# Triangular inverses on 32x32 array tiles, two units per direction in flight, in a one-core encoder layer

## The chip, the core and the metric

The kernel runs on one NeuronCore of a Trainium2 chip. The metric is device time in microseconds (us) of one execution. Engines are named as in the profile: PE (TensorE matmul) and PEld (its weight loads), DVE (VectorE), ACT (ScalarE), POOL (GpSimd), SP (SyncE, which issues the DMAs here).

## The reference

The layer normalises and modulates `x`, projects it once, and splits the projection between a dilated-window attention (three dilations, merged by their softmax denominators) and a bidirectional RWKV-7 time mixing. Both outputs are projected back, and a squared-ReLU feed-forward part follows. It is applied to 2048 prompt tokens and 256 sample tokens, with shared weights, in f32. The part that matters here is the recurrence, run forward and backward for 8 heads of 64:

```python
def _rwkv_step(state, inp):
    w, kk, b, k, v, r = inp
    sa = jnp.einsum('dbhvk,dbhk->dbhv', state, kk)
    state = state * w[..., None, :] - sa[..., :, None] * b[..., None, :] + v[..., :, None] * k[..., None, :]
    y = jnp.einsum('dbhvk,dbhk->dbhv', state, r)
    return state, y
```

The kernel does it in chunks of 64 tokens. Inside a chunk the dependence of each token on the earlier ones is a unit triangular 64x64 system, whose matrix is inverted; between chunks only the 64x64 state is handed on.

## The kernel before, in words

The program has three phases, one after the other: phase A (projection, token shift, decay), phase B (recurrence and attention, interleaved), phase C (output projection and feed-forward). Only phase B is changed. There is one stretch of phase B for each `c` of 0 to 3 (a pair of heads, in the two 64-partition halves).

A *unit* is 8 chunks of one direction `d` of one `c` (the sample tokens form units of 4 chunks): per `c` four units of 8 and one of 4 for each direction, 40 units in all. `units[::2]` are forward, `units[1::2]` backward. A *half* is 4 chunks of both directions; there are 36. For each unit the following run as separate streams, written as Python generators:

- `load_stream`: SP loads the tiles `kr` and `bk` (`NKR` and `NBK` buffers) of the unit.
- `prod_stream`: PE multiplies `bk` by `kr`, 64 partitions at a time (`hd` is the head), four chunks into one PSUM bank named `pb`; `mask_stream` copies it to the tile `x` on ACT, `gate_stream` masks it on POOL. There are `NX` tiles `x`, freed when the unit's chain is done.
- `prep_stream` calls `unit_prep`: the inverse. The 64x64 matrix is seen as 2x2 blocks of 32. Both diagonal blocks are inverted in f16 by five doubling levels (`for li in range(5)`), refined twice, and the off-diagonal block follows from two products in high and low parts. A level is: product on PE into `pb`, mask on DVE (`xs`), second product on PE, update of `t` on DVE, a DVE transpose of 32x32 blocks into `mc`. In each product four blocks (2 heads, 2 diagonal blocks) of each chunk are computed at once with a 128x128 operand that holds the four 32x32 blocks on its diagonal and zeros elsewhere. `spread` makes this operand: a DVE multiplication by a block mask that writes 128 columns per chunk from 32. Its outputs are `mb` and `mbl`; the operands `e32` and `eof`, filled from `x`, are kept spread as well. `low_stream` forms the low parts of these on POOL.
- At the end of `unit_prep` the tile `m` is written (`NLATE` buffers; it waits until the chain of the unit `NLATE` before is done, and `lock2` lets one unit at a time through), and a DMA puts another operand into `x`. Then the unit is marked `ready`.
- `late_load` and `late_gate`: for each half SP loads `rc` and `uv`; POOL scales `bk`, PE transposes it, ACT copies it to `bt`. There are `NH` sets.
- `chain_stream` calls `pair_chain`: 8 (or 4) steps for a forward and a backward unit together. A step is: products into the bank `pc` (`x,uv` and `rc,uv`), copy `rr` on ACT, product `rr,m`, copy into `uv` on ACT, products `uv,bt` and `uv,x`, then the new state on DVE (`uv<-pc,sw`). It starts when both units are `ready`; there are 144 steps.

One `prep_stream` per direction takes its units one after the other, so two inverses are in progress at a time. Beside all this `attn_stream` keeps up to six attention blocks in flight (`ps` scores, `pt` transposes, `pb` outputs), and `norm_stream` finishes the rows of `y`.

The order on each engine is fixed when the program is built. The class `Pace` keeps a model of when each engine is free, with a cost for each operation, and takes next the stream whose next operation can start first, plus a small amount times its progress. The engines then execute in that order and wait for semaphores. Where the model sees PE idle for long, `warm` adds products of the constant `bdh` whose results are overwritten (*fillers* below). The PSUM banks are: three `pb`, two `pc`, two `ps`, one `pt`.

## Time and profile before

| | us |
|---|---|
| median of 3 runs (lowest, highest) | 4227.92 (4219.04, 4238.62) |
| the profiled execution | 4239.46 |
| its span, first to last instruction | 4237.6 |
| first and last chain step in it | 1145.1, 2353.9 |

Mean granted PE clock over the span: 0.962. Over the span PE is busy 95%, DVE 62%, ACT 41%, POOL 35%. Matmuls overlap in a pipeline, and a matmul's busy time is that from its start to its modelled end: eight small products that start 25 ns apart count 0.35 us together, though one alone counts 0.17 us. So a busy PE is not one that could take no more. Nearly all operations are recorded by one helper, at line 117, so operations are told apart by their tile names, `out<-in`.

### The profile page before, as it was taken

The numbers are of one execution on the slowest core, as the hardware profiler recorded it, in microseconds if no ns is written. First come the engines' busy times: TensorE is split into PE (matmuls) and PEld (weight loads), VectorE is DVE, ScalarE is ACT, GpSimd is POOL, SyncE is SP. The second block draws the span as 40 slices with busy tenths as digits, with TensorE's granted clock in tenths as the row PEclk, the third lists the DMA queues.
The fourth block names the chain that finished last, engine by engine and source line by source line (L and its number), as shares of the span: only waits on it lengthen the run. The fifth ranks groups of instructions, "written<-read, shape, count | busy, mean of one in ns | idle before, by whom it ended". The sixth has DMA issues, their size and how long they took to land.

```text
span 4237.6 us, 76554 instructions
## 1 busy us (share of the span) xinstructions
PE 4035.7 (95%) x29994; PEld 3339.5 (79%) x29994; DVE 2606.8 (62%) x5429; ACT 1754.5 (41%) x4301; POOL 1484.1 (35%) x1471
## 2 busy tenths in 40 slices
PE   8989999998899999999999799999999999999997
PEld 5878789888566666666666588889999888889997
DVE  4898788788668768767667354444444464444445
ACT  5556556555565566566465322121221221112221
POOL 2553431211645645645544443112121141112123
PEclk9999999999899899899799899999999999999999
DMA  6566565454433323324222444111111141111112
GB/s 228 205 224 224 173 201 191 152 171 153 145 79 94 106 69 93 110 71 109 83 75 55 155 145 154 41 40 48 42 44 42 53 167 40 40 40 43 48 41 80
DMA packets 341674, 452.57 MB, mean 107 GB/s; under 512 B 152384, under 2 KB 237376, under 8 KB 340288
## 3 DMA queue, kind: packets, MB, share of 16 engines
q1 hardware_dynamic: 340480, 446.98, 32.8%
q8 instruction: 236, 3.87, 0.4%
q14 instruction: 126, 1.03, 0.1%
q10 hardware_dynamic: 832, 0.69, 0.1%
HBM read 319.90 MB, written 127.68 MB: 106 GB/s over the span
## 4 chain that ended last, share of the span: by engine, by line
PE 54%; DVE 4%; issue 1%; ACT 1%; POOL 1%; DMA 0%; POOLq 0%; SPq 0%; DVEq 0%; ACTq 0%
PE p L117 42%; PE pb L117 5%; PE pc L117 3%; PE ps L117 3%; PE pt L117 1%; DVE mb L117 1%; DVE m L117 0%; DMA mx<-scr_mix 0%; DVE uv L117 0%; DVE mc L117 0%; DVE t L117 0%; POOL ya L117 0%; POOL x L117 0%; DVE w L117 0%; DVE p L117 0%
## 5 line engine op out<-in xcount | busy, mean ns | idle before, releaser
L117 DVE TENSOR_TENSOR z<-z 128x384 f32<-128x384 f32 x192 | 190.2, 991 | 591.1 <-ACT gh L117 591.1
L117 DVE TENSOR_TENSOR ya<-ya,p 128x512 f32<-128x512 f32 x540 | 363.9, 687 | 277.5 <-PE p L117 276.5
L117 PE MATMUL pin<-hi,whi 128*128 128x386 f32 (+3 forms) x1512 | 499.4, 330 | 16.6 <-ACT praw L325 8.9
L117 PE MATMUL p<-hi,mh 128*128 128x384 f32 x1536 | 513.3, 334 | 0.0
L117 PE MATMUL p<-hi,ml 128*128 128x384 f32 x1536 | 513.2, 334 | 0.0
L117 PE MATMUL p<-lo,mh 128*128 128x384 f32 x1536 | 513.0, 334 | 0.0
L117 PE MATMUL pin<-hi,wlo 128*128 128x386 f32 (+3 forms) x1512 | 484.6, 320 | 6.3 <-POOL wlo L117 5.1
L117 PE MATMUL pin<-lo,whi 128*128 128x386 f32 (+3 forms) x1512 | 484.0, 320 | 1.2 <-DVE lo L117 1.2
L117 PE MATMUL p<-xn,gh 128*128 128x512 f32 x1152 | 458.9, 398 | 0.0
L117 PE MATMUL p<-mx,gh 128*128 128x512 f32 x1152 | 458.1, 398 | 0.5 <-DVE ya L117 0.5
L117 PE MATMUL p<-mx,gl 128*128 128x512 f32 x1152 | 452.1, 392 | 0.0
L117 POOL TENSOR_TENSOR xn<-x,mx 128x1024 fp32r<-128x1024 f32 x64 | 152.8, 2407 | 653.7 <-ACT mx L117 653.7
L117 ACT ACTIVATE mx<-x 128x1024 fp32r<-128x1024 f32 x64 | 64.3, 1052 | 694.6 <-PE p L117 694.6
L117 POOL TENSOR_TENSOR ml<-x,mh 128x1024 fp32r<-128x1024 f32 x64 | 153.8, 2403 | 556.1 <-ACT mh L117 556.1
L117 PEld LDWEIGHTS pin<-hi,whi 128*128 128x128 f32 x1512 | 292.2, 193 | 30.3 <-ACT praw L325 9.8
L117 PEld LDWEIGHTS pin<-hi,wlo 128*128 128x128 f32 x1512 | 292.6, 193 | 9.3 <-POOL wlo L117 7.0
L117 PEld LDWEIGHTS pin<-lo,whi 128*128 128x128 f32 x1512 | 293.3, 194 | 5.5 <-DVE lo L117 2.7
L117 PEld LDWEIGHTS p<-hi,mh 128*128 128x128 f32 x1536 | 288.3, 188 | 1.5
L117 PEld LDWEIGHTS p<-lo,mh 128*128 128x128 f32 x1536 | 288.3, 188 | 1.3
L117 PEld LDWEIGHTS p<-hi,ml 128*128 128x128 f32 x1536 | 288.3, 188 | 0.0
L117 PE MATMUL ps<-kz,q 128*128 128x512 f32 (+2 forms) x400 | 272.7, 775 | 0.8 <-DVE st L117 0.6
L117 PEld LDWEIGHTS p<-mx,gh 128*128 128x128 f32 x1152 | 215.8, 187 | 56.5 <-DVE ya L117 0.9
(303 smaller groups left out, 8895.8 us busy)
## 6 DMA issues: line engine op xcount, KB each, us to landing
x<-wff SPq DMA_DIRECT2D x128, 512.0 KB
whi<-scr_wp SPq DMA_DIRECT2D x54, 512.0 KB
wlo<-scr_wp SPq DMA_DIRECT2D x54, 512.0 KB
raw<-wada SPq DMA_DIRECT2D x83, 256.0 KB
scr_kr<-kr SPq DMA_DIRECT2D x48, 384.0 KB
scr_bk<-bk SPq DMA_DIRECT2D x48, 384.0 KB
x<-xp SPq DMA_DIRECT2D x32, 512.0 KB
kr<-scr_kr SPq DMA_DIRECT2D x32, 512.0 KB
```

What stands on the lines that cost most here:

```text
L117: return f(out, *a, **k)
```

## The change

It does five things. (1) The four 32x32 blocks of a chunk are no longer spread over a 128x128 operand: the new function `blocks` issues four products, each with a 32x32 stationary operand at the partitions of its block, and its output in the 32 partitions of the same block (or of the neighbouring one, `swap`). `spread`, `mb`, `mbl` and `lock2` go, and `e32` and `eof` have 32 columns a chunk. (2) There are four sets of the inverse's tiles (`u["set"]`), and four `prep_stream`s and `low_stream`s: two units of each direction can be in progress. (3) In `prod_stream` the products of the two heads alternate and fill two `pb` banks. (4) The tile `bk` is freed after these products; `late_gate` works on a tile `bkl` that `late_load` loads again for each half. (5) `NBK, NX, NH, NLATE` go from 3, 5, 3, 3 to 2, 6, 2, 4, and the model's costs know of the small tiles.

```diff
-            if b.dtype == FH:
-                return max(26.0, n / 2.4 + 3), n * rows
+            if b.dtype == FH:
+                return max(26.0, n / 2.4 + 3) * (0.4 if m == 32 else 1.0), n * rows
...
-        NKR, NBK, NX, NH, NLATE, NY = 1, 3, 5, 3, 3, 4
+        NKR, NBK, NX, NH, NLATE, NY = 1, 2, 6, 2, 4, 4
...
+        e32 = [[cp.tile([128, 8, 32], FH, name=f"e32{q}{i}") for i in range(4)] for q in range(2)]
+        eof = [[cp.tile([128, 8, 32], FH, name=f"eof{q}{i}") for i in range(4)] for q in range(2)]
...
                 for n0 in range(0, nn, 4):
+                    yield room("pb", NPB), room("pb", NPB - 1), "P"
+                    u[n0, 0], u[n0, 1] = pbank([128, 4, 128]), take(psB, [128, 4, 128], FT, "pb", NPB)
+                    for n in range(4):
+                        for hd in range(2):
+                            pr = slice(64 * hd, 64 * hd + 64)
+                            mm2(u[n0, hd][0][:, n], bk[pr, n0 + n, :], kr[pr, n0 + n, :], start=True, stop=True)
...
+                    yield room(f"bkl{d}", 1), "S"
+                    h["bkl", d] = take(su, [128, 4, 128], FT, f"bkl{d}", 1)
+                    dma_(h["bkl", d][0], S["bk"][c, d, :, n0:n0 + 4, :])
...
-            def spread(c32, mask, name):
-                z = su.tile([128, 8, 128], FH, name=name, bufs=1)
-                tt(z[:, :nn].rearrange("p n (b t) -> p n b t", b=4), c32[:, :nn, None, :].to_broadcast([128, nn, 4, 32]),
-                   mask[:, None].to_broadcast([128, nn, 4, 32]), OP.mult)
-                return z
...
+            def blocks(ps, w, swap, *pairs):
+
+                for n in range(nn):
+                    for z, (a, b) in enumerate(pairs):
+                        for q in range(4):
+                            r, o = slice(32 * q, 32 * q + 32), slice(32 * (q ^ swap), 32 * (q ^ swap) + 32)
+                            mm(ps[o, n, 0:w], a[r, n], b[r, n], start=z == 0, stop=z == len(pairs) - 1)
...
-                    for n in range(nn):
-                        mm(ps[:, n, 0:16], mb[:, n], xs[:, n], start=True, stop=True)
+                    blocks(ps, 16, 0, (mc, xs))
...
-            yield (lambda: late(u) and not lock2), at_(i - NLATE, "done")
-            lock2.append(i)
-            xlb = spread(xl, bdsw[:, d], "mbl")
-            yield
+            yield (lambda: late(u)), at_(i - NLATE, "done")
...
         def prep_stream(d):
-            for u in units[d::2]:
+            for u in units[d::4]:
...
+            for k in (d, d + 2):
+                pace.add(prep_stream(k), "prep", lambda d=k: prog[1, d] + BT["prep"])
+                pace.add(low_stream(k), "low", lambda d=k: prog[1, d] + BT["low"])
```

The order on DVE, in the middle of an inverse. `t` is the running inverse of a unit, `mc` its transpose, `xs` the masked product, `tpl` the low part in the last stage of the other unit; a number after a name is the buffer. Before:

```order
L117 SCALAR_TENSOR_TENSOR t_14491<-pb,t_14491 128x64x2
L117 STREAM_TRANSPOSE mc_14655<-t_14491 128x256
L117 TENSOR_TENSOR mb_14657<-mc_14655,bdh 128x1024
L117 SCALAR_TENSOR_TENSOR tpl_14637<-pb,tph_14636 128x256
L117 TENSOR_TENSOR mb_14669<-tph_14636,bdh 128x1024
L117 TENSOR_TENSOR mbl<-tpl_14637,bdh 128x1024
L117 TENSOR_TENSOR xs_14704<-pb,lvl 128x128
```

And now:

```order
L117 TENSOR_TENSOR xs_20276<-pb,lvl 128x128
L117 SCALAR_TENSOR_TENSOR m_20282<-t_19332,eyes 128x256
L117 SCALAR_TENSOR_TENSOR mph_20284<-pb,m_20282 128x256
L117 SCALAR_TENSOR_TENSOR o_11176<-o_11176,pv,pb 128x512
L117 SCALAR_TENSOR_TENSOR t_19865<-pb,t_19865 128x32x4
L117 STREAM_TRANSPOSE mc_20345<-t_19865 128x256
L117 TENSOR_TENSOR xs_20397<-pb,lvl 128x128
```

The multiplications by `bdh` into `mb` and `mbl` are gone; what follows a transpose is the next level's `xs` at once.

The order on PE, around a chain step (`rr,m`, then `uv,bt` and `x,uv`). Before:

```order
L117 MATMUL pc<-rr,m 64x64 x4
L117 MATMUL pb<-kr,bk 128x128 x4
L117 MATMUL pc<-uv,bt_13232 64x64 x2
L117 MATMUL pc<-uv,bt_13308 64x64 x2
L117 MATMUL pc<-x,uv 64x64 x4
L117 MATMUL pb<-kr,bk 128x128 x4
```

And now:

```order
L117 MATMUL pb<-kr,bk 128x128 x8
L117 MATMUL pc<-rr,m 64x64 x4
L117 MATMUL pb<-ident,bkl_33228 128x128 x4
L117 MATMUL pc<-uv,bt_32642 64x64 x2
L117 MATMUL pc<-uv,bt_32746 64x64 x2
L117 MATMUL pc<-x,uv 64x64 x4
```

The products `kr,bk` of the two heads, two groups of 4 that stood in different places of a step, are one group of 8.

The order on SP, at the loads for a half. Before:

```order
L181 DMA bk<-scr_bk 128x512
L181 DMA kr<-scr_kr 128x1024
L181 DMA rc_19246<-scr_kr 128x4x64
L181 DMA rc_19280<-scr_kr 128x4x64
L181 DMA vx<-scr_v 64x512
L181 DMA uv<-scr_vt 64x4x64 x4
```

And now:

```order
L185 DMA bkl_26335<-scr_bk 128x512
L185 DMA bkl_26428<-scr_bk 128x512
L185 DMA vx<-scr_v 128x512
L185 DMA rc_26334<-scr_kr 128x4x64
L185 DMA rc_26427<-scr_kr 128x4x64
L185 DMA x<-scr_kr 64x8x64
L185 DMA uv<-scr_vt 64x4x64 x4
```

Two loads `bkl` stand ahead of those of `rc` and `uv` of the same half.

## The prediction, as put on record before the change was run

> **What bounds the kernel now.** I read the chain's steps first, since only phase B changes and a chain of 144 steps runs through it. The copy `rr` on ScalarE occurs once a step, so its starts are the steps' clock. The first fence is the tile view of `rr` (count, durations in ns, first and last start in us), the second the ScalarE timeline over the end of one unit and around a change of `c`.

> ```profile
> L117 ACT ACTIVATE rr<-pc x144: 253/278/322, 1145.1 to 2353.9; 128x128 f32<-128x128 f32 x144
> ```

> ```profile
> 1414.64 0.28 ACT L117 ACTIVATE rr<-pc 128x128 f32<-128x128 f32 x1 [4.37 <-PE pc L117]
> 1440.03 0.27 ACT L117 ACTIVATE rr<-pc 128x128 f32<-128x128 f32 x1
> ...
> 1600.92 0.28 ACT L117 ACTIVATE rr<-pc 128x128 f32<-128x128 f32 x1
> 1610.31 0.26 ACT L117 ACTIVATE rr<-pc 128x128 f32<-128x128 f32 x1
> 1615.83 0.28 ACT L117 ACTIVATE rr<-pc 128x128 f32<-128x128 f32 x1
> 1621.46 0.28 ACT L117 ACTIVATE rr<-pc 128x128 f32<-128x128 f32 x1 [0.17 <-PE pc L117]
> 1634.98 0.28 ACT L117 ACTIVATE rr<-pc 128x128 f32<-128x128 f32 x1
> ```

> The steps take 2353.9 - 1145.1 = 1208.8 us, 8.45 us each. They are not even: within the unit the gaps are 5.5 to 9.4 us, into the next unit 13.5 us (1621.46 to 1634.98), into the next `c` 25.4 us. Summing the 143 gaps of these rows by kind, the 124 within units make 895 us (7.2 each) and the 19 into a next unit 314 us (16.5 each), of which the three into a next `c` (25.4, 31.1, 40.4) make 97. What is waited for at 1634.98 stands in the VectorE timeline of that stretch: the last operation of each inverse (`m<-pb,m`) and the first of the next (`COPY t<-eye`).

> ```profile
> 1607.65 0.39 DVE L117 SCALAR_TENSOR_TENSOR m<-pb,m 128x256 f32<-128x256 f32 x1
> ...
> 1613.66 0.19 DVE L117 COPY t<-eye 128x128 f16<-128x128 f16 x1
> ...
> 1628.32 0.42 DVE L117 SCALAR_TENSOR_TENSOR m<-pb,m 128x256 f32<-128x256 f32 x1
> ...
> 1635.28 0.15 DVE L117 COPY t<-eye 128x128 f16<-128x128 f16 x1
> ```

> The second unit's inverse ends at 1628.7, its last operand is then loaded into `x`, and the chain steps on at 1635. In each direction the next inverse starts only after the one before (1607.65 to 1613.66, 1628.32 to 1635.28). So the two inverses in progress run back to back and finish just before each pair of units can start: at unit boundaries the chain waits for the inverses. The stretch as a whole (windows view: busy us of PE, PEld, DVE, ACT, POOL, then granted clock, DMA share, GB/s):

> ```profile
> 1145.00:2354.00 1209.00, 1151.64 (x14616) 808.87 (x14615) 857.49 (x2699) 708.19 (x2313) 606.11 (x833) 0.93 0.31 85
> ```

> VectorE is busy 71%, ScalarE 59%, POOL 50%. PE's 95% counts pipelined latency.

> **The change, part by part.** The sum is made against the profiled execution, 4239.46 us, which lies 11.5 above the median.

> *Spreading goes.* These groups (lines view) vanish from VectorE:

> ```profile
> L117 DVE TENSOR_TENSOR mb<-mc,bdh 128x1024 f16<-128x1024 f16 (+1 forms) x160 | 127.3, 796 | 5.5
> L117 DVE TENSOR_TENSOR mbl<-tpl,bdh 128x1024 f16<-128x1024 f16 (+1 forms) x40 | 32.9, 822 | 0.1
> L117 DVE TENSOR_TENSOR mb<-mph,bdh 128x1024 f16<-128x1024 f16 (+1 forms) x40 | 29.2, 730 | 1.4
> L117 DVE TENSOR_TENSOR mb<-tph,bdh 128x1024 f16<-128x1024 f16 (+1 forms) x40 | 28.4, 709 | 0.0
> ```

> Together 217.8 us, 1.5 us of each chain step's 8.45, and 7 operations, about 5.4 us, of each inverse. VectorE is not the wait within steps, so this is not 218 us of time. Bounds for the 143 gaps: 0 and -215 (1.5 each).

> *Two units per direction.* An inverse that starts a unit earlier no longer ends last. I let the 16 ordinary boundaries fall from (314 - 97) / 16 = 13.6 us to a step within a unit, 7.2: 16 x 6.4 = **-102**. The three changes of `c` I leave as they are, because attention is drained there too. What the chain's stall gives place to is the step itself; so the late thing next is whichever engine a step queues on.

> *Steps within units.* I take a quarter of the freed VectorE time, 0.37 us a step: **-53**. A quarter, because a step passes VectorE once (`uv<-pc,sw`) and PE four times, and because the two further inverses now compete inside the steps.

> *Fill.* The first inverse is 5 us shorter: **-5**.

> *Small tiles on PE.* These PE timeline rows carry the price (start, time to the modelled end of the last, form, count):

> ```profile
> 1502.22 0.40 PE L117 MATMUL pc<-uv,x 128*64 128x64 f32 x8
> 1502.56 0.45 PE L117 MATMUL pc<-rc,uv 64*64 64x64 f32 x8
> ...
> 1503.87 0.35 PE L117 MATMUL pb<-xs,mb 128*128 128x16 f16 x8
> ...
> 1504.64 0.45 PE L117 MATMUL pc<-rr,m 64*64 64x64 f32 x8
> ```

> ```profile
> 1197.19 1.71 PE L117 MATMUL pb<-kr,bk 64*128 64x128 f32 x16
> 1199.53 1.16 PE L117 MATMUL pb<-kr,bk 64*128 64x128 f32 x8
> ```

> ```profile
> L117 PE MATMUL pb<-t,e 128*128 128x16 f16 (+1 forms) x2016 | 88.0, 173 | 6.7 <-DVE t L117 3.0 <-ACT x L117 2.5 <-ACT e L117 0.6
> L117 PE MATMUL pc<-rr,m 64*64 64x64 f32 x1152 | 68.9, 241 | 2.8 <-ACT rr L117 2.6
> L117 PE MATMUL pb<-kr,bk 64*128 64x128 f32 x1152 | 155.1, 295 | 0.9 <-DMA bk<-scr_bk 0.5 <-ACT x L117 0.2 <-DVE mph L117 0.2
> ```

> A full-width f16 product starts every (0.35 - 0.17) / 7 = 25.6 ns. There are 144 per unit of 8 chunks, 5184 in all; each becomes four. No 32x32 product is in the trace. From below, four abreast cost one, 25.6 ns; from above, four in turn cost 102 ns. The nearest row is `rr,m`, whose two heads sit on the two diagonal 64x64 tiles: (0.45 - 0.24) / 7 = 30 ns a matmul, where a 128-column matmul on one tile (`kr,bk` x8) costs (1.16 - 0.295) / 7 = 124, so 62 for 64 columns. Two tiles thus run about twice abreast. I take 31 ns for four: 5184 x 5.4 = +28 us of PE time; at 102 it is +396.

> *Products `kr,bk`.* 1152 matmuls at 0.11 us are 127 us of PE. With the heads alternating, pairs may run abreast: the x16 row, in which two heads meet once, adds 0.55 us for its second 8 where 0.88 is the cost alone. Bounds 0 and -63; I take -50.

> *Fillers.* Counted in PE's order, the program had 354 filler products and has 198 now; at 0.17 us (below, three started in 0.66) that is -26 us of PE.

> ```profile
> 1302.08 0.66 PE L117 MATMUL pc<-bdh 128*128 128x384 f16 x3
> ```

> PE's own sum is 28 - 50 - 26 = -48 us, 0.3 a step; I count it within the -53.

> *`bkl` and fewer sets.* 72 loads of 256 KB come in. A half now needs load, scaling, transposes and copy after the half two before is done:

> ```profile
> L117 POOL TENSOR_TENSOR bk<-bk,wc 128x512 f32<-128x512 f32 x72 | 81.8, 1140 | 5.9 <-PE pb L117 3.1
> L117 ACT ACTIVATE bt<-pb 128x512 f32<-128x512 f32 x72 | 42.7, 596 | 38.9 <-PE pb L117 37.8
> ```

> At 85 GB/s for a 31% share the DMA engines would move 256 KB in about 1 us (an estimate); with 1.14, some 0.5 for four transposes and 0.6 it is 3.3 us, against the 4 x 7.2 = 29 us of the half that the chain is in meanwhile. So nothing; without that cover, 36 x 3.3 = +119. Behind the loads in SP's queue stand `rc`, `uv`, and the loads of the next units.

> *Instructions.* The page's row of the DMA queue that fetches instructions (packets, MB, share of 16 engines):

> ```profile
> q8 instruction: 236, 3.87, 0.4%
> ```

> PE's 60,000 instructions (29994 and 29994 on the page) took 236 fetches of 256; 31,104 more are 121 more, in about 1.15 us each (0.4% of 16 engines' span over 236). Phase B's matmuls (x14616 in the windows row, and as many weight loads) took 114, so with these some 235 over 1050 us, one per 4.5 us, fetched ahead: 0; if PE stood for each, +139.

> **Sum:** -102 - 53 - 5 = -160, so 4079.5 for an execution like the profiled one and **4068** against the median.

> **The rivals.** *(A) The steps shrink too.* Two of the three gaps shown within a unit are 5.5 and 5.6 us, so steps of 6 us do happen, with two inverses and attention beside them. With everything at 6: 143 x 6 + 3 x 20 for the changes of `c` = 918, a gain of 290: 3938. Against it: PE's, ScalarE's and POOL's work per step stays.

> *(B) Work is only moved.* The boundary gaps are not idle; PE is 95% busy over the stretch, attention filling them. If each engine's time is conserved, moving the inverses into the steps lengthens these, and only PE's own -48 and the fill remain: 4175. For it: the gaps of 5.5 and 5.6 us are the last of their unit, when the inverses are nearly through. Against it: PE's busy time is latency, and VectorE, the fullest besides, loses a quarter.

> *(C) Slower: the tiles take turns.* PE's instructions for the inverses quadruple. At 102 ns PE gains 396 - 76 = +320 us of work, more than the boundaries return: with -102 and -5, +213, 4441. It decides from about 25.6 + (160 + 76) / 5.184 = 71 ns per four. Against it stands `rr,m`.

> [...]

> **How the numbers follow.** Forecast 0.54; A 0.15; B 0.17; C 0.09; no change 0.05 (halves or banks now hold the chain where inverses did). Each case's place: 4068 with its own range 4010 to 4130 (step term 0 to -110); 3938; 4175; 4441; 4228. The range leaves out C and the better half of A: 3950 to 4200. A measurement here can tell 0.5%, 21 us, from no change: faster 0.54 + 0.15 + 0.17 = 0.86, same 0.05, slower 0.09.

> **What would show it.** Inverses: `m<-pb,m` of a pair ends a step or more before the chain's first `rr`, and `COPY t<-eye` of the next unit of a direction starts before it; if not, the -102 is wrong. Steps: 144 `rr` spread over 1020 to 1060 us with boundary gaps like the others; with B, gaps of 8 us throughout. Tiles: a group of 32 small products lasts 0.35 to 0.45 us for C to be wrong; at 0.9 or more C is right. Loads: `rr` gaps at every fourth step longer than the rest would mean that `bt` is late. Waits of PE on nothing, inside groups of small tiles, would mean instruction fetches.

## The result

The changed kernel takes 4355.02 us (median of 4 runs, 4351.93 to 4355.6) against 4229.18 for the kernel before in the same comparison (4 runs, 4219.04 to 4238.62): 1.0297 times as long, 95% interval 1.0272 to 1.0321. The forecast was 4068 us and the range 3950 to 4200. It was wrong, and in the sign.

First the tile view of `rr` in the changed kernel: count, durations in ns, first and last start in us.

```profile
L117 ACT ACTIVATE rr<-pc x144: 254/277/310, 1152.3 to 2454.6; 128x128 f32<-128x128 f32 x144
```

The chain's 144 steps take 1302.3 us instead of 1208.8: 93.5 of the 115.4 us by which the profiled span grew (4353.0 against 4237.6). Of the other 22, 7 lie before the first step and 15 behind the last; these were not followed further.

Sorted as in the prediction, the 19 gaps into a next unit fell from 314 to 238 us, and the 124 within units rose from 895 to 1064 (7.2 to 8.6 us each). The inverses do end early, as these VectorE and ScalarE rows of the changed kernel show, from the end of one pair of inverses to the steps behind it, and the first step that uses the pair:

```profile
1640.94 0.42 DVE L117 SCALAR_TENSOR_TENSOR m<-pb,m 128x256 f32<-128x256 f32 x1 [2.30 <-PE pb L117]
1645.88 0.42 DVE L117 SCALAR_TENSOR_TENSOR m<-pb,m 128x256 f32<-128x256 f32 x1 [2.01 <-PE pb L117]
```

```profile
1640.52 0.27 ACT L117 ACTIVATE rr<-pc 128x128 f32<-128x128 f32 x1
1651.14 0.25 ACT L117 ACTIVATE rr<-pc 128x128 f32<-128x128 f32 x1
1661.94 0.28 ACT L117 ACTIVATE rr<-pc 128x128 f32<-128x128 f32 x1
...
1687.68 0.27 ACT L117 ACTIVATE rr<-pc 128x128 f32<-128x128 f32 x1
```

These two inverses belong to the units whose first step is at 1687.7, 42 us later. Over the 19 boundaries the later `m<-pb,m` comes 21 to 58 us ahead of the first step it serves, where it came 3 to 23 us ahead before. But the steps beside it last 10.6 and 10.8 us.

The next two fences are the windows view of that stretch (span, busy us of PE, PEld, DVE, ACT, POOL, granted clock, DMA share, GB/s) and PE's waits in it (us in total, times, longest).

```profile
1152.00:2455.00 1303.00, 1184.21 (x29038) 804.60 (x29034) 664.47 (x2429) 703.10 (x2319) 571.60 (x827) 0.85 0.34 93
```

```profile
PE pb L117 <- issue: 60.0, 51, 4.0
PE pc L117 <- issue: 11.8, 8, 2.5
```

VectorE lost 193 us of work, as the diff promises. Three new things stand beside that. PE has 29038 matmuls for 14616. The granted clock fell from 0.93 to 0.85; the clock's records in the two traces (102 and 72) show full or half speed only, and half speed for 395 us of the chain's span instead of 163. And PE waits 71.8 us for "issue", that is, for nothing that the profile shows; the same view of the kernel before has no such row. The PE timeline shows one of these waits:

```profile
1481.68 0.20 PE L117 MATMUL pb<-xs,mc 32*32 32x16 f16 x3
1485.45 0.36 PE L117 MATMUL pb<-xs,mc 32*32 32x16 f16 x29 [3.57 <-issue]
```

A group of 32 small products stops after the third, for 3.6 us, while no operand is missing. The queue that fetches instructions is where to look next (packets, MB, share of 16 engines, in the window of each kernel's chain; the changed kernel first, then the kernel before):

```profile
q8 instruction: 228, 3.74, 1.2%
```

```profile
q8 instruction: 115, 1.88, 0.6%
```

The groups of small products in the same stretch (lines view, forms apart: busy us, mean ns of one, idle us before them and what ended it) show where the waits fall; before, the full-width `xs,mb` and `t,e` (16 columns) had 8.4 and 6.7 us of idle time before them, on operands:

```profile
L117 PE MATMUL pb<-t,e 32*32 32x16 f16 x5440 | 64.8, 168 | 8.9 <-issue 6.7 <-DVE t L117 2.0
L117 PE MATMUL pb<-xs,mc 32*32 32x16 f16 x4352 | 53.6, 169 | 18.6 <-issue 14.4 <-DVE xs L117 2.9 <-ACT bt L117 0.5
L117 PE MATMUL pb<-t,e 32*32 32x32 f16 x2240 | 25.6, 180 | 14.6 <-issue 14.1 <-DVE m L117 0.3 <-DVE t L117 0.2
```

In this window 58,072 matmuls and weight loads came in 228 fetches, 255 for each; over the whole trace, with PE's waits on semaphores, it is 91,306 instructions in 356 fetches of 16,384 bytes, 256 for each, and 60,384 in 236, again 256, in the kernel before. I counted the gaps of PE longer than 150 ns after which the next instruction waits on no semaphore and starts 1.15 to 1.75 us after the end of such a fetch: 125 gaps, 99.6 us together; in the kernel before 21 gaps and 4.4 us. This sum depends on what is called a gap, and it takes in some chance. If only time behind the modelled end of the last product counts, there are 58 gaps without a wait, 69.9 us, and the kernel before has none; from start to start of the products there are 171, 107 us, against 63 and 15.

The 58 strict gaps show the cause. After every one of them PE resumes 1.18 to 1.63 us behind the end of a fetch. Counted in PE's order of instructions, all 58 lie at the same place modulo 256, to one instruction: at the seam between two fetches. And the trace's chain of work that ended last, which runs through all of this stretch, goes through 69 of the 69.9 us. So the time was lost, and not only idle.

When does a seam stall? In all the traces of this case no two fetches start less than 3.2 us apart (3.30 in the changed kernel, 6.48 in the kernel before). In the changed kernel PE used up 59 of the 228 blocks of 256 instructions in less than 3.3 us, and 46 of these ended in a stall; of the 169 others, 12 did. The kernel before took 6 us or more over every block of its chain.

### The profile page after: what moved, and what is told of

It is laid out like the page before. It is cut to its first block, busy times and chain, and to the rows that moved or that the text cites. A ratio compares the mean times of both kernels' runs of the same rounds, so it can differ in the third digit from the quotient of the medians.

```text
span 4353.0 us, 107383 instructions
## 1 busy us (share of the span) xinstructions
PE 4072.4 (94%) x45412; PEld 3335.4 (77%) x45412; DVE 2403.4 (55%) x5149; ACT 1746.5 (40%) x4301; POOL 1441.3 (33%) x1471
## 4 chain that ended last, share of the span: by engine, by line
PE 65%; issue 4%; DVE 3%; ACT 2%; POOL 1%; DMA 1%; SPq 0%; POOLq 0%; DVEq 0%; ACTq 0%
PE p L117 41%; PE pb L117 11%; PE pc L117 6%; PE ps L117 6%; PE pt L117 2%; DVE w L117 0%; POOL x L117 0%; DVE uv L117 0%; DMA mx<-scr_mix 0%; POOL ysq L117 0%; POOL ya L117 0%; ACT x L117 0%; ACT uv L117 0%; DMA kr<-scr_kr 0%; ACT p L117 0%
## 5 line engine op out<-in xcount | busy, mean ns | idle before, releaser
L117 DVE TENSOR_TENSOR ya<-ya,p 128x512 f32<-128x512 f32 x540 | 363.7, 687 | 277.9 <-PE p L117 276.9
L117 DVE TENSOR_TENSOR z<-z 128x384 f32<-128x384 f32 x192 | 190.0, 990 | 592.0 <-ACT gh L117 592.0
L117 PE MATMUL pin<-hi,whi 128*128 128x386 f32 (+3 forms) x1512 | 499.6, 330 | 15.8 <-ACT praw L329 10.2
L117 PE MATMUL p<-hi,mh 128*128 128x384 f32 x1536 | 513.3, 334 | 0.0
L117 PE MATMUL p<-hi,ml 128*128 128x384 f32 x1536 | 513.2, 334 | 0.0
L117 PE MATMUL p<-lo,mh 128*128 128x384 f32 x1536 | 513.1, 334 | 0.0
L117 PE MATMUL pin<-hi,wlo 128*128 128x386 f32 (+3 forms) x1512 | 484.5, 320 | 6.4 <-POOL wlo L117 5.5
L117 PE MATMUL pin<-lo,whi 128*128 128x386 f32 (+3 forms) x1512 | 483.8, 320 | 0.7 <-DVE lo L117 0.7
L117 PE MATMUL p<-xn,gh 128*128 128x512 f32 x1152 | 458.9, 398 | 0.0
L117 PE MATMUL p<-mx,gh 128*128 128x512 f32 x1152 | 458.1, 398 | 0.5 <-DVE ya L117 0.5
L117 PE MATMUL p<-mx,gl 128*128 128x512 f32 x1152 | 452.1, 392 | 0.0
L117 POOL TENSOR_TENSOR xn<-x,mx 128x1024 fp32r<-128x1024 f32 x64 | 152.7, 2406 | 653.5 <-ACT mx L117 653.5
L117 ACT ACTIVATE mx<-x 128x1024 fp32r<-128x1024 f32 x64 | 64.3, 1051 | 694.6 <-PE p L117 671.0
L117 POOL TENSOR_TENSOR ml<-x,mh 128x1024 fp32r<-128x1024 f32 x64 | 153.8, 2403 | 556.7 <-ACT mh L117 556.6
L117 PEld LDWEIGHTS pin<-hi,whi 128*128 128x128 f32 x1512 | 292.2, 193 | 29.7 <-ACT praw L329 11.4
L117 PEld LDWEIGHTS pin<-hi,wlo 128*128 128x128 f32 x1512 | 292.4, 193 | 9.8 <-POOL wlo L117 7.8
L117 PEld LDWEIGHTS pin<-lo,whi 128*128 128x128 f32 x1512 | 293.2, 194 | 4.6 <-DVE lo L117 1.9
L117 PEld LDWEIGHTS p<-hi,mh 128*128 128x128 f32 x1536 | 288.3, 188 | 1.5
L117 PEld LDWEIGHTS p<-lo,mh 128*128 128x128 f32 x1536 | 288.3, 188 | 1.3
L117 PEld LDWEIGHTS p<-hi,ml 128*128 128x128 f32 x1536 | 288.3, 188 | 0.0
L117 PE MATMUL ps<-kz,q 128*128 128x512 f32 (+2 forms) x400 | 283.9, 806 | 0.7 <-DVE st L117 0.7
L117 PEld LDWEIGHTS p<-mx,gh 128*128 128x128 f32 x1152 | 215.8, 187 | 56.4 <-DVE ya L117 0.9
```

The source lines that it names most:

```text
L117: return f(out, *a, **k)
```

## The experiments

All have the chain's span from the `rr` rows, which I use beside the times, since it is what the change moves. "Boundaries" is the sum of the 19 gaps into a next unit, "step" the mean of the other 124, "half speed" the time in the chain at half the clock, "fetch stalls" the first of the sums above (125 gaps in the changed kernel), "changes" the number of times that PE goes from one tiling (rows x columns of the array) to another.

| | us, ratio to before [interval] | chain | boundaries | step | half speed | fetch stalls | changes |
|---|---|---|---|---|---|---|---|
| before | | 1208.8 | 314 | 7.22 | 163 | 4 | 1560 |
| changed | 4355, 1.0297 [1.0272, 1.0321] | 1302.3 | 238 | 8.58 | 395 | 100 | 1771 |
| e1_wide | 4126, 0.9739 [0.9723, 0.9756] | 1090.6 | 193 | 7.24 | 76 | 5 | 1465 |
| e2_one | 4325, 1.0227 [1.0206, 1.0248] | 1278.3 | 225 | 8.49 | 338 | 103 | 1757 |
| e3_act | 4371, 1.0323 [1.0307, 1.0339] | 1325.3 | 249 | 8.68 | 328 | 78 | 2214 |
| e4_extra | 4478, 1.0575 [1.0557, 1.0593] | 1416.1 | 351 | 8.59 | 370 | 27 | 2275 |
| e5_thin | 4176, 0.9881 [0.9864, 0.9897] | 1153.0 | 198 | 7.70 | 227 | 8 | 1792 |
| e6_wide1 | 4134, 0.9777 [0.9761, 0.9793] | 1104.0 | 195 | 7.33 | 99 | 7 | 1484 |
| e7_late4 | 4353, 1.0296 [1.0280, 1.0312] | 1317.1 | 241 | 8.68 | 418 | 9 | 2110 |
| e8_hyb2 | 4179, 0.9880 [0.9862, 0.9898] | 1141.7 | 180 | 7.75 | 150 | 25 | 1677 |
| e9_group | 4293, 1.0153 [1.0126, 1.0180] | 1262.3 | 231 | 8.32 | 350 | 8 | 1642 |
| e10_kr | 4222, 0.9985 [0.9972, 0.9998] | 1203.8 | 348 | 6.90 | 205 | 8 | 1526 |
| e11_hyb2act | 4180, 0.9884 [0.9864, 0.9904] | 1152.9 | 175 | 7.89 | 123 | 25 | 1676 |
| e12_wide3 | 4167, 0.9856 [0.9834, 0.9877] | 1148.1 | 334 | 6.57 | 131 | 5 | 1471 |
| e13_hyb5 | 4212, 0.9957 [0.9941, 0.9973] | 1179.7 | 187 | 8.01 | 229 | 23 | 1576 |
| e14_hyb6 | 4206, 0.9947 [0.9931, 0.9963] | 1178.5 | 233 | 7.62 | 174 | 7 | 1627 |
| e15_afteract | 4347, 1.0275 [1.0253, 1.0298] | 1296.1 | 187 | 8.95 | 379 | 91 | 1762 |

The column of fetch stalls is for comparing runs. By the strict count it is 70 us for the changed kernel, 71 for e2_one, 49 for e3_act, 65 for e15_afteract, 14, 13 and 10 for e8_hyb2, e11_hyb2act and e13_hyb5, 8 for e4_extra, and nothing for the others. e1_wide, e5_thin, e6_wide1 and e12_wide3 leave the inverse out of the result, so they are measures of time alone.

The theory after the result was: the early inverses bring what was forecast, and the small tiles take it back, by instruction fetches and by a slower clock. The rival: the four sets and the second unit in flight crowd the steps, whatever the tiles are.

### Small tiles or the rest: e1_wide

In the changed kernel, one full-width product per chunk from the compact operand (four chunks' operands side by side as 128 columns) stands in place of four small ones. Wherever its result is used it is scaled by zero; the second pair of lines is one of seven such places.

```diff
-                        for q in range(4):
-                            r, o = slice(32 * q, 32 * q + 32), slice(32 * (q ^ swap), 32 * (q ^ swap) + 32)
-                            mm(ps[o, n, 0:w], a[r, n], b[r, n], start=z == 0, stop=z == len(pairs) - 1)
+                        m0 = min(n, nn - 4)
+                        mm(ps[:, n, 0:w], a[:, m0:m0 + 4].rearrange("p n t -> p (n t)"), b[:, n], ...)
...
-                    stt(sel[:, :nn], x4(ps), -2.0 ** -8, sel[:, :nn], OP.mult, OP.add)
+                    stt(sel[:, :nn], x4(ps), 0.0, sel[:, :nn], OP.mult, OP.add)
```

> The changed kernel with each group of four small products replaced by one full-width product that takes four neighbouring compact blocks as its 128 columns. The results are wrong, so every use of them is scaled by zero: the inverse is left out, and everything else (two units per direction, the waits, VectorE's work) stays. PE's instructions for the inverse go back to a quarter, and each product covers the whole array. Theory F (PE runs dry of instructions) and theory K (small tiles count little as activity, so the clock gate halves PE's clock) both expect the loss to go: 4060 to 4160 us, half clock at most 200 us in phase B, gaps without a wait that end 1.2 to 1.7 us after an instruction fetch under 15 us in all (97 us in the changed kernel). Theory Q (four inverses at once crowd the chain's steps) expects it to stay: above 4300 us.

```profile
1134.00:2224.00 1090.00, 1046.91 (x14544) 726.85 (x14541) 656.81 (x2434) 699.54 (x2326) 577.68 (x832) 0.97 0.40 111
```

4126 us, 212 us of chain less than the changed kernel. Everything but the tiles is worth -118 us of chain; the tiles cost the 212. The rival falls as the account of the loss; e2_one below shows that with small tiles the second unit costs 24 us.

### What of the tiles costs: e5_thin

As e1_wide, but only 32 rows of the operands are used: the same number of products and streamed columns, a quarter of the array's area, and a tiling (32x128) that differs from that of the work around it. The planner was told to count such a product like a full-width one, so that it plans as for e1_wide (185 fillers in both).

```diff
-                        mm(ps[:, n, 0:w], a[:, m0:m0 + 4]..., b[:, n], ...)
+                        mm(ps[:, n, 0:w], a[0:32, m0:m0 + 4]..., b[0:32, n], ...)
```

> The run with full-width products of the compact blocks (inverse left out, results scaled by zero), but each product uses only the first 32 partitions of its operands: as few instructions as there, and a quarter of the array's area per product, as the small tiles have. Theory K (the clock gate sees too little activity) expects half clock in phase B to rise from 76 us to 300 or more and the time from 4126 to 4250 us or more. Theory F (instructions run short) expects 4110 to 4170 us, half clock at most 150 us, stalls after fetches under 10 us.

```profile
1120.00:2273.00 1153.00, 1117.15 (x14552) 757.98 (x14548) 655.86 (x2436) 703.52 (x2326) 578.77 (x833) 0.90 0.38 105
```

Neither expectation had 4176 us with 227 us at half speed: it lies just above the one and far below the other. From e1_wide to e5_thin the chain grows by 62 us, and the clock falls from 0.97 to 0.90 with as many instructions. From e5_thin to the changed kernel, where each product becomes four and the area stays, it grows by another 149, while fetch stalls grow by 92, by the strict count by 70. (The planner counts 41.6 ns for four small products and 26 for one, so the two orders are not quite the same.) What the rest is, 57 or 79, was not isolated; half-speed time grows by 168 us in the same step.

### Instructions without small area, and area without fewer instructions: e4_extra, e3_act

e4_extra is the kernel before with three idle small products behind each product of an inverse; e3_act is the changed kernel with full-width products behind each group that stream the columns which the array lost.

```diff
+            def idle(ps, k):
+                for n in range(nn):
+                    for _ in range(k):
+                        for q in range(3):
+                            r = slice(32 * q, 32 * q + 32)
+                            nc.tensor.matmul(ps[r, n, 48:64], bdh[r, 0, q], bdh[r, 0, q, 0:16], start=True, stop=True)
```

> The kernel before with three small products of a constant behind each of its 5184 full-width products of the inverse, in unread columns of the same bank: as many instructions as in the changed kernel, no less activity, the same order of everything else. F expects stalls after fetches of 80 us or more and 4310 to 4400 us. K expects no such stalls and 4230 to 4290 us (some of about 145 us of added PE time shows).

```diff
+                left = 3 * nn * w * len(pairs) // 4
+                while left > 0:
+                    k = min(left, 32 * nn) // nn
+                    nc.tensor.matmul(ps[:, :nn, 32:32 + k], bdh[:, 0]..., bdh...[:, :nn * k], ...)
+                    left -= nn * k
```

> The changed kernel with PE's activity put back: behind each group of small products full-width products of a constant, whose columns make up the three quarters of array area that the small tiles leave out; nothing reads their results. About 1300 instructions more and some 40 us of PE time. K expects half clock in phase B to fall from 406 us to 200 or less and the time to 4240 to 4290 us. F expects no gain, 4350 to 4400 us, with the stalls after fetches still near 100 us.

Neither is a clean test, and e4_extra's 4478 us lies above both its expectations. In e4_extra the idle groups stand on the inverses' own path, at 0.3 us each, and bring 715 changes of tiling; the chain grew by 207. It says one thing: 229 fetches come in, as in the changed kernel, yet fetch stalls are 27 us, not 100. The number of fetches alone doesn't set the stall; how fast PE uses a block up does. In the changed kernel the median group of 32 small products has 31 gaps in 0.199 us, 6.4 ns a product with its weight load: 256 instructions would last 0.82 us at this pace, where fetches start 3.2 us apart at best (one takes 1.2% x 16 x 1303 / 228 = 1.1 us of that). In e4_extra, whole groups of full-width products lie between, and 15 blocks were used up in less than 3.3 us where the changed kernel has 59. In e3_act half-speed time fell by 67 us and fetch stalls by 22, but 443 changes of tiling and the extra columns came in: 1.0323, the same as or a little worse than the change.

### The second unit in flight: e2_one, e6_wide1

The changed kernel, and e1_wide, with one `prep_stream` per direction.

```diff
-            for u in units[d::4]:
+            for u in units[d::2]:
...
-            for k in (d, d + 2):
+            for k in (d,):
```

> The changed kernel with one unit per direction in flight again (two streams of inverses, not four); small tiles and all else stay. Theory Q expects a gain over the changed kernel, 4150 to 4230 us, with steps within units back near 7.2 us. F and K expect it to be as slow as the changed kernel or slower, 4340 to 4420 us: the same instructions, less to fill PE, half clock 400 us or more.

> The run with full-width products of the compact blocks (inverse left out, results scaled by zero), with one unit per direction in flight. Theory I (the second unit in flight is what shortens the waits at unit boundaries) expects the 19 boundaries back near 300 us in all and 4200 to 4240 us. Theory M (the fourth tile m is: before, the last product of a pair's second unit had to wait for the chain of the pair before) expects 4110 to 4150 us and boundaries near 200 us, as with two.

e2_one's 4325 us lies between its expectations. With small tiles one unit in flight is 24 us of chain better than two; with full-width products it is 13 worse. Boundaries hardly move (238 to 225, 193 to 195). So the second unit in flight is not what empties them.

### What empties the boundaries: e12_wide3, e7_late4, e10_kr

e12_wide3 is e1_wide with three tiles `m`, the inverses' outputs, instead of four.

```diff
-        NKR, NBK, NX, NH, NLATE, NY = 1, 2, 6, 2, 4, 4
+        NKR, NBK, NX, NH, NLATE, NY = 1, 2, 6, 2, 3, 4
```

> e1_wide (one full-width product from compact operands in place of four small ones, results scaled by 0, so that the inverse is left out) with three m tiles instead of four. Theory M (the fourth m tile lets the second inverse of a pair end in time): boundaries rise by 50 to 73 us from 193, 4175 to 4200. Theory S (the spreads' removal shortens the inverses, and the m tile does not matter): 4120 to 4140.

```profile
L117 ACT ACTIVATE rr<-pc x144: 253/277/331, 1126.1 to 2274.2; 128x128 f32<-128x128 f32 x144
```

The boundaries go back to 334 us: the fourth `m` moved them, by 141. But the steps go from 7.24 to 6.57 us, 83 us in all. The chain pays only 57. The waits at a boundary were not idle: what is taken out of them lengthens the steps beside it. Neither expectation gave 4167; it lies between them.

e7_late4 was to show the same in the kernel before. There is no room for a fourth `m` there, so the low part `el` was kept compact and its product cut into four small ones, each set behind a full-width product of the high part.

```diff
-        NKR, NBK, NX, NH, NLATE, NY = 1, 3, 5, 3, 3, 4
+        NKR, NBK, NX, NH, NLATE, NY = 1, 3, 5, 3, 4, 4
...
                 mm(ps[:, n, 0:32], eh[:, n], t[:, n], start=True, stop=False)
-                mm(ps[:, n, 0:32], el[:, n], t[:, n], start=False, stop=True)
+                for q in range(4):
+                    r = slice(32 * q, 32 * q + 32)
+                    mm(ps[r, n, 0:32], el[r, n], t[r, n], start=False, stop=True)
```

> The kernel before with four tiles m instead of three (NLATE 4). The 2 KB for it come from keeping the low parts of the diagonal blocks compact; their one product, 8 of an inverse's 144, runs as 32 small tiles. Nothing else of the change. M expects boundaries down from 314 to about 220 us and 4120 to 4170 us. I expects them to stay at 290 or more and 4220 to 4250 us.

The boundaries fell by 73, and yet it took 4353 us. No theory had that, and its own edit was the cause in part: see e9_group.

e10_kr is the kernel before with the two heads' `kr,bk` products in turn (part 3 of the change).

> The kernel before with part 3 of the change alone: the kr,bk products of the two heads alternate and fill two pb banks; everything else is as before. If the pairs run abreast and PE counts inside the steps: 1152 products at 78 instead of 119 ns are 47 us of PE, half of it or all on the path: 4180 to 4205. If the pairs run abreast but PE is not what the steps wait for, or if taking two of the three pb banks at once holds the inverses back: 4225 to 4260.

PE's `kr,bk` products start at a mean of 69 ns from one to the next for 119 (78 in the changed kernel), and the steps are shorter (6.90), but the boundaries are longer by 34: 4222, no change. So the term for `kr,bk` was right on PE and worth nothing in time.

### A change of tiling: e9_group

In e7_late4 the refinement alternates between the full-width product of `eh` and four small ones of `el`, eight times. e9_group issues all of the first, then all of the second, with the rest of the program as it was.

```diff
                 mm(ps[:, n, 0:32], eh[:, n], t[:, n], start=n == 0, stop=False)
+            for n in range(nn):
                 for q in range(4):
```

> The kernel of e7_late4 with one loop split: all full-width products of the high part first, then all 32x32 products of the low part, in the same PSUM accumulation. Same instructions, same plan; only the 8 alternations per group become one. In e7's trace a product starts 25 ns after one of the same tiling, and 124 to 126 ns after one of the other tiling (272 and 237 such pairs). Theory 'drain' (a change between full-width and 32x32 tiling costs PE about 97 ns): some 475 of the 544 changes vanish, 46 us of PE in phase B; the chain gets 40 to 60 us shorter, 4290 to 4315 us, and still above before, because what else e7 lost is the granted clock (half of full speed for 418 us against 163). Theory 'amplified' (PE is the bound in the steps and the drains are what lowered the clock): 4150 to 4230, since the boundaries had already fallen by 73. Theory 'four m tiles make a bad plan' (drains lie beside other work): 4340 to 4365, unchanged.

The PE timeline of e7_late4 first, then of e9_group, each at two such refinements in a row, 16 full-width and 64 small products:

```profile
1327.31 4.29 PE L117 MATMUL pb<-t,e 128*128 128x32 f16 x80
```

```profile
1303.66 1.27 PE L117 MATMUL pb<-t,e 128*128 128x32 f16 x80
```

The same 80 products take 3.0 us less with 28 changes fewer, 0.11 us each. In the starts of e7_late4, 1160 pairs of full-width products lie 25 ns apart at the median, 272 pairs full-width to small 120, 237 pairs small to full-width 118, and 816 pairs of small ones of one chunk 3. The whole program gained 60 us (4353 to 4293), the chain 55: 468 changes at 0.095 (120 - 25 ns) are 44, and half-speed time fell by 68 us with them.

So theory "drain" held, at 0.1 us a change. It leaves a rest: e9_group is still 1.5% slower than before, with 350 us at half speed and 120 fillers in the chain's span where the kernel before has 306. The next runs look at that rest.

### Mixtures: e8_hyb2, e11_hyb2act, e13_hyb5, e14_hyb6

e8_hyb2 is the changed kernel with one unit per direction and with `e32` and `eof` block-diagonal as before (they are filled from `x` without extra work); only the operands that VectorE had to spread run on small tiles.

```diff
+                        if a.shape[-1] == 128:
+                            mm(ps[:, n, 0:w], a[:, n], b[:, n], start=z == 0, stop=z == len(pairs) - 1)
+                            continue
                         for q in range(4):
```

> The changed kernel with one unit per direction in flight and the operands taken from x spread over 128 columns again (ScalarE and POOL write them, at no more cost), so that their 80 products of an inverse are full-width; only the 64 whose operands VectorE had to spread run as small tiles. 336 products of an inverse instead of 576, 144 before. F expects stalls after fetches of 30 to 60 us (100 in the changed kernel) and 4180 to 4270 us; if the count of instructions is not it, the time stays where small tiles with one unit per direction were, 4325 us.

```profile
L117 ACT ACTIVATE rr<-pc x144: 252/278/338, 1131.8 to 2273.5; 128x128 f32<-128x128 f32 x144
```

```profile
1132.00:2273.00 1141.00, 1088.08 (x20993) 753.95 (x20987) 654.59 (x2432) 703.64 (x2318) 578.75 (x835) 0.93 0.38 105
```

4179 us, 1.2% faster than before, with 20993 matmuls for 29038, a clock of 0.93 and 25 us of fetch stalls. Of the kernels here that compute the whole function, it is, with e11_hyb2act, the fastest.

e11_hyb2act is e8_hyb2 with another count for the clock in the planner: a 32x32 product counts a quarter of what it did.

```diff
-                return max(26.0, n / 2.4 + 3) * (0.4 if m == 32 else 1.0), n * rows
+                return max(26.0, n / 2.4 + 3) * (0.4 if m == 32 else 1.0), n * rows * (0.25 if m == 32 else 1.0)
```

> The kernel of e8_hyb2 with one number of the planner changed: a 32x32 product counts with a quarter of what it counted towards the activity by which the planner foresees a slow clock, as the granted clock of the traces weighs it (rows times columns of the array). The planner will then put in more fillers. If the clock is what e8 still loses (150 us at half speed, against 76 in e1_wide): half-speed time below 120 us and 4155 to 4172. If the fillers stand in the way of the chain or the clock does not follow: 4175 to 4200.

There are 170 fillers for 138 and 27 us less at half speed; the time is the same.

e13_hyb5 and e14_hyb6 take e8_hyb2 and bring spreads on VectorE back: the first those of the levels (`mc`), the second those of the inverse's end (`r0`, `xh`, `xl`). Both halve the small products.

> The kernel of e8_hyb2 with the level operands mc spread over 128 columns on VectorE again (four spreads of 0.8 us per inverse); r0, xh and xl stay on 32x32 tiles. Small products per inverse of 8 chunks fall from 256 in 6 groups to 128 in 2. Theory K (the 45 us by which e8 stands behind e6_wide1 are the price of small products: changes of tiling, fetches, issue): half of it comes back, 4150 to 4168. Theory V (four m tiles pay only while VectorE has no level spreads between the chain's steps, as e9_group's loss suggests): steps of 8.2 us and more, 4200 to 4290.

> The kernel of e8_hyb2 with r0, xh and xl spread on VectorE again (three spreads, 2.3 us per inverse, at its end, the last one behind a lock that lets one unit at a time through); the levels stay on 32x32 tiles: 128 small products in 4 groups per inverse in place of 256 in 6. Theory K: a third to a half of the 45 us comes back, 4155 to 4170. Theory V (spreads in the way of the steps): these three are fewer and stand at the end, where they lengthen the inverse by 2.3 us: 4180 to 4215.

Windows rows of e13_hyb5 and of e14_hyb6:

```profile
1124.00:2300.00 1176.00, 1103.59 (x17832) 764.61 (x17830) 768.90 (x2573) 702.15 (x2309) 603.50 (x834) 0.90 0.37 103
```

```profile
1124.00:2300.00 1176.00, 1104.09 (x17857) 760.89 (x17856) 746.72 (x2557) 703.75 (x2327) 597.80 (x837) 0.93 0.37 103
```

Both windows start some 10 us before the chain and end 11 to 15 us before it does; over the chain itself VectorE's work differs by 1 to 3 us from what they give. Both lose: 38 and 37 us of chain for 114 and 92 us of VectorE's work beyond e8_hyb2's. The times are those of theory V, though e13_hyb5's steps, 8.01 us, stay short of its 8.2: VectorE's spreads do stand in the chain's way, at a third of a microsecond for each. That is no clean price, since fewer small products should have helped, and half-speed time grew by 79 and 24 us. It fits e9_group, where all spreads and four `m` meet, but that sum was not measured by itself.

### The clock's own price: e15_afteract

The changed kernel with e11_hyb2act's line.

> The changed kernel with one number of the planner changed: a 32x32 product counts a quarter of what it counted towards the activity by which the planner foresees a slow clock, as the granted clock of the traces weighs it; more fillers follow. Theory 'the clock has its own price' (0.2 to 0.4 us of chain per us at half speed, from e5_thin against e1_wide): half-speed time falls from 395 to below 340 and the time to 4325 to 4345. Theory 'the clock follows from the stalls' (PE is too often without instructions to be kept busy, and fillers only add work): 4350 to 4375, half-speed time about as before.

The planner put in fewer fillers, 129 for 158, and not more, because the order moved too. Half-speed time stayed (379 for 395) and so did the time within the intervals. The run doesn't tell the two theories apart.

## Why the prediction was wrong

The differences of the chain along one path, each between two runs that are in the table:

| step | us of chain |
|---|---|
| before to e12_wide3: no spreads, compact operands, two in flight, `kr,bk` in turn, `bkl` (three `m`) | -60.7 |
| to e1_wide: the fourth `m` | -57.5 |
| to e5_thin: a quarter of the area, changes of tiling | +62.4 |
| to the changed kernel: four instructions for one | +149.3 |
| sum | +93.5 |

*Two units per direction, -102.* The rows showed the boundaries waiting for inverses, and this was so: the inverses now end 21 to 58 us early. The size was off and the cause misnamed. A boundary gap was priced as if the steps stayed at 7.2 us. Emptying 141 us of boundary (e12_wide3 to e1_wide) put 83 back into the steps, as rival B had it in part, and the fourth `m`, listed among the buffers and given no price, did it; the second unit in flight is worth 13 at best.

*Steps within units, -53.* As a price for VectorE's spreads it was about right: 0.25 us per us was taken, and e13_hyb5 and e14_hyb6 show 0.33 and 0.40, the clock's share included. In the changed kernel it is covered by what PE lost.

*Small tiles, +28.* Their own pace was read rightly, and rival C was wrong: this row of the changed kernel is a group of 32.

```profile
1489.26 0.36 PE L117 MATMUL pb<-t,e 32*32 32x16 f16 x32
```

Four cost 6.4 x 4 = 26 ns at the median, a little below the 31 that were taken. What the term lacked is the array, in two ways. It has nothing for a change of tiling. In the prediction's rows `rc,uv` (64x64) starts at 1502.56, before the end of `uv,x` (128x64) at 1502.62, and no price can be read from that. But the ends are modelled, and the starts should have been compared: in the kernel before, over the 144 steps, the first `rc,uv` starts 152 ns behind the last `uv,x` at the median, where two `uv,x` start 43 ns apart on average. In the changed kernel small products follow small ones at 6 ns at the median, and what follows in another tiling starts 97 to 109 ns after the last of them. That makes 0.1 us a change; the net number of changes rose by only 211, some 20 us. And the term held nothing for the clock: four 32x32 products give the array a quarter of the area of the product they replace, and the clock fell, from 0.97 to 0.90 where e5_thin cut the area (with as many instructions, and 327 more changes of tiling).

*Instructions, 0; if PE stood for each, +139.* This is the step that failed by most. The count was right (228 fetches forecast as 235), and the bound was not passed; the choice between 0 and 139 was made by the mean rate, one fetch per 4.5 us (5.7 in the run), and by my assumption, with no figure beside it, that instructions are fetched ahead. The kernel before bears it out, with 115 fetches in its chain and no gap by the strict count; the changed kernel doesn't. The small products come in groups: 59 of the 228 blocks were used up in less than 3.3 us, where fetches follow each other at 3.2 us at best over all traces, and 46 of them ended in a stall. The trace gives 70 us of stalls, 69 of them on the chain that ended last (by the first count 92 more than e5_thin's), of the 149. No run takes the fetches alone away. The sign by which it would show was named, and it came: PE's waits on nothing, inside groups of small tiles.

*`kr,bk`, fillers, `bkl`, 0 in time.* e10_kr bears out the first: the products came 50 ns closer together, from 119 ns, and the time stayed (the prediction priced one at 0.11 us where its own rows give 124 ns). Nothing in the runs speaks against the others; `bkl` was not tried alone.

Open is the clock's own price. Between the kernel before and the changed one, half-speed time grows by 232 us. e1_wide to e5_thin bounds it: 151 us more at half speed and 327 more changes of tiling cost 62 us; with 0.095 for a change (measured between full-width and 32x32, taken over for 32x128), 31 are left, 0.2 us for each at half speed. At that price the clock would be some 46 of the changed kernel's loss, an estimate. e11_hyb2act gained nothing from 27 us less.

## What to carry to other kernels

When an edit multiplies small instructions, price the fetch at the burst and not at the mean: cut the engine's order into blocks of one fetch (256 instructions in these traces), and hold the time of the densest blocks against the closest spacing of fetches that a trace shows, which is longer than one fetch takes (3.2 us for 1.1 here). The kernel before could not show that spacing, since its own fetches start 6.5 us apart or more; the changed kernel's trace does, with 3.3 us. Price a shorter wait at a boundary only by what the work that filled it would cost elsewhere. And change only what a spread, a copy or another real cost had to pay for: the mixture that put just the spread operands on small tiles and left the free block-diagonal ones alone gained 1.2% where the whole change lost 3%.
